# Stick-breaking attention weights: sigmoid(z) times a scanned product of sigmoid(-z), in place of exp(z minus a running sum of softplus)

## The chip, the cores and the metric

The kernel runs on one core of a Trainium2 chip. The metric is the device time of one execution in microseconds (us); less is better. A core has five engines that run beside each other and synchronise by semaphores: TensorE (PE, matrix products, with its own queue of weight loads, PEld), VectorE (DVE), ScalarE (ACT), GpSimd (POOL) and SyncE (SP, which issues the DMAs). Each engine runs its instructions in a fixed order.

## The reference

Two transformer-like blocks follow each other on 1024 tokens of width 1024, in float32. The second block projects its input to ten parts, among them q, k, v of a stick-breaking attention with 8 heads of width 128, and q, k, v of a retention; both results are gated, projected, merged and projected again. Only the stick-breaking attention matters here:

```python
z = jnp.einsum('bhqd,bhkd->bhqk', qi, k).astype(jnp.float32) * scale
qpos = i * Q_BLOCK + jnp.arange(Q_BLOCK)
mask = kpos[None, :] < qpos[:, None]
log_keep = jnp.where(mask, jax.nn.log_sigmoid(-z), 0.0)
suffix = lax.cumsum(log_keep, axis=3, reverse=True) - log_keep
w = jnp.where(mask, jnp.exp(jax.nn.log_sigmoid(z) + suffix), 0.0)
return jnp.einsum('bhqk,bhkd->bhqd', w.astype(v.dtype), v)
```

A query t gives the key s < t the weight sigmoid(z[t,s]) times the product of (1 - sigmoid(z[t,j])) over the keys j between s and t. Before attention q and k are normalised per head.

## The kernel before

The program is one long function, `tile_kernel`, written in the order of the computation; a scheduler with its own timeline then fixes the order of the instructions on every engine, so that work of neighbouring heads interleaves. Nearly every product is made of three passes, since float32 operands are split into a high and a low part: high x high, high x low, low x high (`PASSES`).

**The stages.** The first block takes the first part of the span. Then comes the stick-breaking stage, a loop over 8 heads, then one group of merge logits (`merge_logits(0)`), the retention with its own projections, the other merge logits, and the three final projections.

**A head of the stick-breaking stage** has two parts. The first is its projection: 8 weight tiles are loaded and split (`split_unit`: L67 and L68 on ACT and DVE for one half of the tiles, L70 and L71 on POOL for the other). `dense_tok` (L102) makes q, k and v for one block of 128 tokens after the other, 24 matmuls each of 384 columns, in a PSUM tile `acc`; there are three such banks. For every block of tokens ACT squares q and k with a running sum (L983), POOL makes the power -1/2 (`rsqrt_small`, L125 and L126), ACT and DVE split v (L986, L987) and DVE scales q and k into `sq` (L989). After four blocks PE transposes q and k (L996, eight transpositions into two of the `acc` banks), and ACT and DVE split the result into `qkt` (L1000, L1001). The gate of the head comes by `dense_col` (L112, 48 matmuls of 512 columns), or for head 0 in L1006.

The second part is attention proper, for two halves (`ib`) of 512 queries. The first half has four blocks on the diagonal, of 128, 256, 384 and 512 keys; the second half has four such blocks, and four off the diagonal with 512 keys each: 12 blocks in a head, 96 in all. For each block PE makes the logits `pz` (L1026, in one of two banks), ACT, DVE and POOL make the weights in the tile `A` (L1030 to L1051). They compute max(z, 0) + ln(1 + exp(-|z|)), which is softplus(z), its running sum from the last key to the first (the scan, L1042, whose start for off-diagonal blocks is a column `ini` of the diagonal one, L1046), then z minus that sum, and exp. On the diagonal a select sets the masked part, once before the scan and once after. When four blocks are there PE transposes the weights, in four groups by keys (L1058, into the banks `pt` and `pp` in turn), ACT casts a group to its high part (L1060), DVE subtracts it from the original for the low part (L1061), both called `wT`, and PE adds three products of the group to the output `po` (L1063), the first and third with the high part, the second with the low one. DVE copies `po` out (L1067).

The lines that the change touches:

```python
e1 = nc.scalar.activation(out=A[:, :w], in_=pz[:, :w], func=AF.Abs)
nc.scalar.copy(out=Z[:, :w], in_=pz[:, :w])
nc.scalar.activation(out=A[:, :w], in_=A[:, :w], func=AF.Exp, scale=-1.0)
nc.scalar.activation(out=A[:, :w], in_=A[:, :w], func=AF.Ln, bias=1.0)
```

ACT holds one set of function tables at a time. The program loads by hand the set with exp and ln (`load6`, L962), ordered behind the last SiLU of the first block; other loads are put in automatically where a function needs them.

## Time and profile before

| | |
|---|---|
| median of 3 runs | 2317.09 us (2314.77 to 2318.42) |
| the profiled execution | 2316.85 us |
| its span, first to last instruction | 2315.1 us |
| mean granted TensorE clock | 0.984 of full speed |
| PE busy | 2182.2 us, 94% of the span |
| DVE, POOL, ACT busy | 1242.6, 1210.2, 879.1 us (54%, 52%, 38%) |

The profile is of one execution. An engine's busy time is the sum of its instructions' time, overlaps counted once; its idle time is put down to what released the waiting instruction. Matmuls are pipelined, so that several are under way at a time: what one adds to the time is the distance from start to start, which is shorter than its duration. The granted clock of a stretch is a share of full speed, 2.4 GHz; the only other level is 1.2 GHz, so a share between 0.5 and 1 mixes the two. The stick-breaking stage lies at about 870 to 1437 us of the span.

### The profile page before, as it was taken

How to read it: one execution, taken by the hardware profiler on the slowest of the kernel's cores; microseconds unless marked ns; L12 is line 12 of the kernel's file. 1: busy time of each engine (PE TensorE's matmuls, PEld its weight loads, DVE VectorE, ACT ScalarE, POOL GpSimd, SP SyncE). 2: the span in 40 equal slices, each digit the busy share in tenths (PEclk: the TensorE clock that was granted, in tenths of full speed). 3: DMA queues.
4: the chain of work that ended last, by engine and by line, in shares of the span. 5: the costliest groups of instructions: out<-in, count | busy, mean ns of one | idle time of the engine just before them, and what ended most of it. 6: DMA issues, size and time to landing. Idle time of an engine off the chain costs nothing.

```text
span 2315.1 us, 33643 instructions
## 1 busy us (share of the span) xinstructions
PE 2182.2 (94%) x12197; PEld 1875.5 (81%) x12197; DVE 1242.6 (54%) x2228; ACT 879.1 (38%) x2191; POOL 1210.2 (52%) x1435
## 2 busy tenths in 40 slices
PE   7998888899999988999999999999989999999999
PEld 7777877787898778988888888788878788788887
DVE  4688789844457555665566453327474744321221
ACT  5344434445544225565566544012222222321200
POOL 6667778762004345554565545536575754434531
PEclk9999999999999999999999999999999999999999
DMA  4266830054486431110111103221324333644433
GB/s 129 83 165 166 206 86 26 35 159 130 146 280 215 147 106 42 55 47 23 51 51 55 51 32 97 67 69 55 125 87 132 95 105 101 218 164 152 142 106 107
DMA packets 238791, 249.25 MB, mean 108 GB/s; under 512 B 40032, under 2 KB 173856, under 8 KB 238368
## 3 DMA queue, kind: packets, MB, share of 16 engines
q1 hardware_dynamic: 238624, 247.10, 34.0%
q8 instruction: 96, 1.57, 0.3%
q14 instruction: 71, 0.58, 0.1%
HBM read 171.51 MB, written 75.53 MB: 107 GB/s over the span
## 4 chain that ended last, share of the span: by engine, by line
PE 43%; POOL 7%; DVE 7%; issue 4%; DMA 3%; ACT 3%; SPq 0%; POOLq 0%; ACTq 0%
PE acc L112 26%; PE acc L102 9%; PE acc L859 3%; POOL wu L71 2%; DMA raw<-in_w_in_dram 2%; PE po L1063 2%; DVE A L1042 1%; POOL wu L70 1%; DVE A L1037 1%; POOL A L1047 1%; PE pt L1179 1%; POOL ss L126 1%; ACT A L1036 1%; DVE xo L909 1%; DVE kf L132 1%
## 5 line engine op out<-in xcount | busy, mean ns | idle before, releaser
L112 PE MATMUL acc<-h2h,wu 128*128 128x512 f32 x1504 | 460.5, 396 | 0.7 <-POOL wu L71 0.4
L102 PE MATMUL acc<-wu,h2h 128*128 128x384 f32 (+1 forms) x1536 | 374.5, 326 | 11.5 <-DVE v L1117 5.5
L71 POOL TENSOR_TENSOR wu<-raw,wu 128x512 fp32r<-128x512 f32 (+3 forms) x268 | 364.9, 1370 | 6.1
L70 POOL TENSOR_SCALAR wu<-raw 128x512 fp32r<-128x512 f32 (+3 forms) x268 | 206.3, 773 | 269.1 <-PE acc L112 187.9
L112 PEld LDWEIGHTS acc<-h2h,wu 128*128 128x128 f32 x1504 | 281.8, 188 | 65.2 <-POOL wu L71 0.8
L102 PEld LDWEIGHTS acc<-wu,h2h 128*128 128x128 f32 x1536 | 270.4, 192 | 18.4 <-DVE v L1117 6.3
L112 PE MATMUL acc<-h2l,wu 128*128 128x512 f32 x752 | 277.9, 395 | 0.0
L102 PE MATMUL acc<-wu,h2l 128*128 128x384 f32 (+1 forms) x768 | 248.2, 324 | 0.0
L102 PE MATMUL acc<-wu,h1hi 128*128 128x384 f32 (+2 forms) x768 | 192.2, 334 | 12.7 <-DVE kS L518 6.7
L112 PE MATMUL acc<-h1hi,wu 128*128 128x512 f32 x512 | 164.5, 409 | 7.3 <-ACT pad L315 3.7
L112 PEld LDWEIGHTS acc<-h2l,wu 128*128 128x128 f32 x752 | 141.3, 188 | 31.0
L102 PEld LDWEIGHTS acc<-wu,h1hi 128*128 128x128 f32 x768 | 137.3, 195 | 17.0 <-issue 8.0
L102 PEld LDWEIGHTS acc<-wu,h2l 128*128 128x128 f32 x768 | 147.5, 192 | 1.3
L1047 POOL TENSOR_TENSOR A<-Z,A 128x128 f32<-128x128 f32 (+2 forms) x96 | 111.3, 1165 | 66.3 <-DVE A L1042 48.4
L125 POOL TENSOR_SCALAR ss<-ss 128x2 f32<-128x2 f32 (+2 forms) x136 | 40.7, 300 | 200.4 <-ACT sq L983 144.0
L102 PE MATMUL acc<-wu,h1lo 128*128 128x384 f32 (+2 forms) x384 | 126.8, 333 | 0.0
L112 PEld LDWEIGHTS acc<-h1hi,wu 128*128 128x128 f32 x512 | 98.2, 194 | 32.3 <-ACT pad L315 5.4
L126 POOL TENSOR_TENSOR ss<-ss,mhalf 128x2 f32<-128x2 f32 (+2 forms) x136 | 113.5, 835 | 8.3
L112 PE MATMUL acc<-h1lo,wu 128*128 128x512 f32 x256 | 96.2, 405 | 0.0
L1037 DVE SCALAR_TENSOR_TENSOR A<-Z,A 128x128 f32<-128x128 f32 (+2 forms) x96 | 70.4, 742 | 42.7 <-ACT A L1036 41.8
L1063 PE MATMUL po<-wT,v 128*128 128x512 f32 (+3 forms) x288 | 76.2, 362 | 14.0 <-DVE wT L1061 11.0
L320 DVE SCALAR_TENSOR_TENSOR cv<-pad,c_conv_w,cv 128x1024 f32<-128x1024 f32 x48 | 76.6, 1597 | 1.1
(549 smaller groups left out, 4685.1 us busy)
## 6 DMA issues: line engine op xcount, KB each, us to landing
raw<-in_w_in_dram SPq DMA_DIRECT2D x192, 256.0 KB, 3.0
d_pk<-sct SPq DMA_DIRECT2D x24, 512.0 KB, 4.3
raw<-in_w_out_dram SPq DMA_DIRECT2D x40, 256.0 KB, 2.9
wsa<-d_pk SPq DMA_DIRECT2D x16, 512.0 KB, 6.1
wsb<-d_pk SPq DMA_DIRECT2D x16, 512.0 KB, 7.1
d_sg<-lg SPq DMA_DIRECT2D x32, 256.0 KB, 2.9
sg<-d_sg SPq DMA_DIRECT2D x32, 256.0 KB, 3.4
raw<-in_w_in_dram SPq DMA_DIRECT2D x32, 192.0 KB, 2.7
```

The costliest lines, as they stand in the source:

```text
L70: nc.gpsimd.tensor_scalar(out=u[:, 0, :], in0=raw, scalar1=1.0, scalar2=0.0, op0=ALU.mult, op1=ALU.add)
L71: nc.gpsimd.tensor_tensor(out=u[:, 1, :], in0=raw, in1=f32(u[:, 0, :]), op=ALU.subtract)
L102: nc.tensor.matmul(acc[:, :n], lhsT=hT[a][:, k, m * P:(m + 1) * P], rhs=us[k][:, b, c0:c0 + n], start=(k == 0 and i == 0), stop=(k == NK - ...
L112: nc.tensor.matmul(accs[half], lhsT=us[k][:, b, c0:c0 + P], rhs=hT[a][:, k, half * 512:(half + 1) * 512], start=(k == 0 and i == 0), stop= ...
L125: nc.gpsimd.tensor_scalar(out=dst, in0=src, scalar1=mul, scalar2=eps, op0=ALU.mult, op1=ALU.add)
L126: nc.gpsimd.tensor_tensor(out=dst, in0=dst, in1=mhalf[:, :eshape], op=ALU.pow)
L132: nc.vector.transpose(out=dst[32 * b:32 * b + 32, :, :, 32 * a:32 * a + 32], in_=src[32 * a:32 * a + 32, :, :, 32 * b:32 * b + 32])
L320: nc.vector.scalar_tensor_tensor(out=cv, in0=pad[:, i:i + T], scalar=conv_w[:, blk, i:i + 1], in1=cv, op0=ALU.mult, op1=ALU.add)
L859: nc.tensor.matmul(acc, lhsT=us[k][:, y, (b % 4) * P:(b % 4 + 1) * P], rhs=token_set(mT[x][:, k, 0:T], s), start=(k == 0 and i == 0), stop ...
L1037: nc.vector.scalar_tensor_tensor(out=A[:, :w], in0=Z[:, :w], scalar=0.0, in1=A[:, :w], op0=ALU.max, op1=ALU.add)
L1047: nc.gpsimd.tensor_tensor(out=A[:, :w], in0=Z[:, :w], in1=A[:, :w], op=ALU.subtract)
L1063: nc.tensor.matmul(po[:, i0 * P:512], lhsT=v[a][:, c0 // P + kb, :], rhs=wT[b][:, :n], start=(diag and kb == 0 and x == 0), stop=(diag == ...
```

## The change

A block's weights are made from two sigmoids of the logits: `A` = sigmoid(-z) and `B` = sigmoid(z), each in one ACT pass out of PSUM. The tile `A` is one column longer, and POOL fills that column with 1. The scan now multiplies from the last key to the first (with a minimum against the same element, which changes nothing, as factors are at most 1), so that column s + 1 of `A` holds the product over the keys behind s; DVE multiplies `B` with it. The selects on the diagonal now set 1 in `A` and 0 in `B`, both before the scan. `A` has three buffers and `B` six, in place of six of `A` and three of `Z`. The manual table load is gone.

```diff
--- before.py
+++ after.py
@@ -959,9 +959,6 @@
     d_oa = dram.tile([8, P, T], F32, name="d_oa")
     d_ga = dram.tile([8, P, T], F32, name="d_ga")
     d_oag = dram.tile([8, P, T], F32, name="d_oag")
-    load6 = nc.scalar.add_instruction(mybir.InstLoadActFuncSet(name=nc.get_next_instruction_name(), act_func_set_id=6,
-                                                               ins=[], outs=[]))
-    after(load6, last_na[0])
     last_sb = None
     with tc.tile_pool(name="sb", bufs=1) as sb, tc.tile_pool(name="sr", bufs=1, side="right") as sr:
         gqk = sr.tile([P, 2, P], F32, name="gqk")
@@ -1026,30 +1023,25 @@
                             nc.tensor.matmul(pz[:, :w], lhsT=qk[0][a][:, i * P:(i + 1) * P], rhs=qk[1][b][:, c0:c0 + w],
                                              start=(x == 0), stop=(x == 2))
 
-                        A = sb.tile([P, 512], F32, tag="A", name="A", bufs=6)
-                        e1 = nc.scalar.activation(out=A[:, :w], in_=pz[:, :w], func=AF.Abs)
+                        A = sb.tile([P, 516], F32, tag="A", name="A", bufs=3)
+                        B = sb.tile([P, 512], F32, tag="B", name="B", bufs=6)
+                        e1 = nc.scalar.activation(out=A[:, :w], in_=pz[:, :w], func=AF.Sigmoid, scale=-1.0)
                         if h == 0:
-                            after(e1, load6)
-                        Z = sb.tile([P, 512], F32, tag="Z", name="Z", bufs=3)
-                        nc.scalar.copy(out=Z[:, :w], in_=pz[:, :w])
-                        nc.scalar.activation(out=A[:, :w], in_=A[:, :w], func=AF.Exp, scale=-1.0)
-                        nc.scalar.activation(out=A[:, :w], in_=A[:, :w], func=AF.Ln, bias=1.0)
-                        nc.vector.scalar_tensor_tensor(out=A[:, :w], in0=Z[:, :w], scalar=0.0, in1=A[:, :w],
-                                                       op0=ALU.max, op1=ALU.add)
+                            after(e1, last_na[0])
+                        last_sb = nc.scalar.activation(out=B[:, :w], in_=pz[:, :w], func=AF.Sigmoid)
+                        nc.gpsimd.memset(A[:, w:w + 1], 1.0)
                         if diag:
-                            nc.gpsimd.affine_select(out=A[:, w - P:w], in_=A[:, w - P:w], pattern=[[-1, P]],
-                                                    compare_op=ALU.is_gt, fill=0.0, base=0, channel_multiplier=1)
-                        nc.vector.tensor_tensor_scan(out=A[:, :w][:, ::-1], data0=A[:, :w][:, ::-1],
-                                                     data1=A[:, :w][:, ::-1], initial=0.0 if diag else ini[:, i4:i4 + 1],
-                                                     op0=ALU.add, op1=ALU.max)
+                            for t_, fill in ((A, 1.0), (B, 0.0)):
+                                nc.gpsimd.affine_select(out=t_[:, w - P:w], in_=t_[:, w - P:w], pattern=[[-1, P]],
+                                                        compare_op=ALU.is_gt, fill=fill, base=0, channel_multiplier=1)
+
+                        nc.vector.tensor_tensor_scan(out=A[:, :w + 1][:, ::-1], data0=A[:, :w + 1][:, ::-1],
+                                                     data1=A[:, :w + 1][:, ::-1], initial=1.0 if diag else ini[:, i4:i4 + 1],
+                                                     op0=ALU.mult, op1=ALU.min)
                         if diag and ib:
                             nc.vector.tensor_copy(out=ini[:, i4:i4 + 1], in_=A[:, 0:1])
-                        nc.gpsimd.tensor_tensor(out=A[:, :w], in0=Z[:, :w], in1=A[:, :w], op=ALU.subtract)
-                        if diag:
-                            nc.gpsimd.affine_select(out=A[:, w - P:w], in_=A[:, w - P:w], pattern=[[-1, P]],
-                                                    compare_op=ALU.is_gt, fill=NEG, base=0, channel_multiplier=1)
-                        last_sb = nc.scalar.activation(out=A[:, :w], in_=A[:, :w], func=AF.Exp)
-                        As.append(A)
+                        nc.vector.tensor_tensor(out=B[:, :w], in0=B[:, :w], in1=A[:, 1:w + 1], op=ALU.mult)
+                        As.append(B)
                     for kb in range(4):
                         i0 = kb if diag else 0
                         n = (4 - i0) * P
```

The scheduler gives the stick-breaking stage a new order on every engine; ahead of it ACT's table loads differ in one place, and behind it no order changes. In the rows below the names are those of the tiles, and a line of the changed kernel is up to eight lower than the same line before (L996 is L993, L1058 is L1050, L1061 is L1053, L1063 is L1055).

PE, where q and k of the first four token blocks of head 5 are transposed, among the output products of head 4's second half. `po<-wT,v` is an output product, `pt` and `pp` are transpositions of weights, `acc<-ident,sq` transpositions of q and k. Before:

```order
L102 MATMUL acc<-wu,h2l 128x384
L996 MATMUL acc<-ident,sq 128x128 x2
L1063 MATMUL po<-wT,v 128x512 x3
L1063 MATMUL po<-wT,v 128x384
L1058 MATMUL pt<-ident,A 128x128 x2
L1063 MATMUL po<-wT,v 128x384 x2
L1058 MATMUL pp<-ident,A 128x128
L996 MATMUL acc<-ident,sq 128x128 x4
L1063 MATMUL po<-wT,v 128x256 x3
L1058 MATMUL pt<-ident,A 128x128 x3
L1063 MATMUL po<-wT,v 128x128
L996 MATMUL acc<-ident,sq 128x128 x2
```

In the changed kernel:

```order
L102 MATMUL acc<-wu,h2l 128x384
L1055 MATMUL po<-wT,v 128x256 x2
L1055 MATMUL po<-wT,v 128x128
L1050 MATMUL pt<-ident,B 128x128
L1055 MATMUL po<-wT,v 128x128 x2
L1050 MATMUL pt<-ident,B 128x128 x3
L1050 MATMUL pp<-ident,B 128x128 x4
L993 MATMUL acc<-ident,sq 128x128 x6
L1055 MATMUL po<-wT,v 128x512 x4
L1050 MATMUL pt<-ident,B 128x128 x4
L993 MATMUL acc<-ident,sq 128x128 x2
L102 MATMUL acc<-wu,h2h 128x384 x2
```

Before, two groups of output products (512 and 384 columns) and part of a third stand between the first and the last transposition of q and k; now it is one product group and the first product of the next, and the groups of 256 and 128 columns stand ahead.

DVE at the same place: `wT<-pt,wT` and `wT<-pp,wT` are the low parts for which the second product of a group waits, `A<-A,ini` is the scan of an off-diagonal block, `A<-Z,A` the combination to softplus, `B<-B,A` the new multiplication. Before:

```order
L1037 SCALAR_TENSOR_TENSOR A<-Z,A 128x512
L1042 SCALAR_TENSOR_TENSOR A<-A,ini 128x512
L1037 SCALAR_TENSOR_TENSOR A<-Z,A 128x512
L1061 TENSOR_TENSOR wT<-pt,wT 128x512
L1042 SCALAR_TENSOR_TENSOR A<-A,ini 128x512
L1061 TENSOR_TENSOR wT<-pp,wT 128x384
L987 TENSOR_TENSOR v<-acc,v 128x128
L989 SCALAR_TENSOR_TENSOR sq<-acc,ss,gqk 128x128 x2
L1037 SCALAR_TENSOR_TENSOR A<-Z,A 128x512
L987 TENSOR_TENSOR v<-acc,v 128x128
L1061 TENSOR_TENSOR wT<-pt,wT 128x256
L1042 SCALAR_TENSOR_TENSOR A<-A,ini 128x512
```

In the changed kernel:

```order
L1038 SCALAR_TENSOR_TENSOR A<-A,ini 128x513
L1043 TENSOR_TENSOR B<-B,A 128x512
L984 TENSOR_TENSOR v<-acc,v 128x128
L1053 TENSOR_TENSOR wT<-pt,wT 128x256
L986 SCALAR_TENSOR_TENSOR sq<-acc,ss,gqk 128x128 x2
L1053 TENSOR_TENSOR wT<-pp,wT 128x128
L984 TENSOR_TENSOR v<-acc,v 128x128
L1053 TENSOR_TENSOR wT<-pt,wT 128x512
L986 SCALAR_TENSOR_TENSOR sq<-acc,ss,gqk 128x128 x2
L1053 TENSOR_TENSOR wT<-pp,wT 128x512
L1053 TENSOR_TENSOR wT<-pt,wT 128x512
L998 TENSOR_TENSOR qkt<-acc,qkt 128x512 x2
```

Before, scans and combinations alternate with the low parts, and the next row is `sq` of the fourth token block; now the two last scans and multiplications come first, and behind the low part of 256 columns no scan follows.

ACT at the first logits of head 0. Before:

```order
L1009 COPY gv<-acc 128x512
L1030 ACTIVATE A<-pz 128x128
L1034 COPY Z<-pz 128x128
L1030 ACTIVATE A<-pz 128x256
L1034 COPY Z<-pz 128x256
L1035 ACTIVATE A<-A 128x128
L67 CAST wu<-raw 128x512
L1035 ACTIVATE A<-A 128x256
L1036 ACTIVATE A<-A 128x128
L1036 ACTIVATE A<-A 128x256
```

In the changed kernel:

```order
L1006 COPY gv<-acc 128x512
L1028 ACT_TABLE_LOAD
L1028 ACTIVATE A<-pz 128x128
L1031 ACTIVATE B<-pz 128x128
L1028 ACTIVATE A<-pz 128x256
L1031 ACTIVATE B<-pz 128x256
L67 CAST wu<-raw 128x512 x2
L1028 ACTIVATE A<-pz 128x384
L1031 ACTIVATE B<-pz 128x384
```

A table load stands ahead of the first sigmoid. In the first block, behind the last SiLU, the change has an automatic load ahead of an Exp (L563) where the manual one stood.

## Rows read from the trace of the kernel before

**Rows 1.** Page, part 1: busy us (share of the span) and instructions.
```profile
span 2315.1 us, 33643 instructions
...
PE 2182.2 (94%) x12197; PEld 1875.5 (81%) x12197; DVE 1242.6 (54%) x2228; ACT 879.1 (38%) x2191; POOL 1210.2 (52%) x1435
```

**Rows 2.** Stretches: from:to, length, busy us of each engine, clock, DMA, GB/s.
```profile
870.00:1437.00 567.00, 536.78 (x2917) 484.41 (x2916) 316.45 (x571) 322.94 (x949) 305.06 (x421) 0.99 0.15 47
...
885.00:900.00 15.00, 15.00 (x83) 13.96 (x82) 7.71 (x11) 8.07 (x22) 11.32 (x14) 1.00 0.43 127
...
1134.60:1203.90 69.30, 65.48 (x366) 59.78 (x365) 39.79 (x74) 40.82 (x123) 36.91 (x53) 1.00 0.15 46
```

**Rows 3.** Waits of PE, 850 to 1450 us: us in total, times, longest.
```profile
PE acc L996 <- DVE sq L989: 13.8, 11, 4.9
PE po L1063 <- DVE wT L1061: 11.0, 14, 1.4
PE pz L1026 <- ACT Z L1034: 4.1, 7, 0.8
```

**Rows 4.** Timeline of PE, head 5: start, us, instruction, [idle before, releaser].
```profile
1198.22 0.90 PE L1063 MATMUL po<-wT,v 128*128 128x512 f32 x3 [0.98 <-DVE wT L1061]
...
1199.87 0.62 PE L1063 MATMUL po<-wT,v 128*128 128x384 f32 x2 [0.52 <-DVE wT L1061]
...
1200.43 0.70 PE L996 MATMUL acc<-ident,sq 128*128 128x128 f32 x4
...
1201.92 0.51 PE L1063 MATMUL po<-wT,v 128*128 128x256 f32 x2 [0.68 <-DVE wT L1061]
...
1203.35 0.59 PE L996 MATMUL acc<-ident,sq 128*128 128x128 f32 x2 [0.54 <-DVE sq L989]
```

**Rows 5.** Timeline of the other engines at the same place.
```profile
1195.73 1.30 POOL L1047 TENSOR_TENSOR A<-Z,A 128x512 f32<-128x512 f32 x1 [2.01 <-DVE A L1042]
...
1195.94 1.63 DVE L1037 SCALAR_TENSOR_TENSOR A<-Z,A 128x512 f32<-128x512 f32 x1 [0.36 <-ACT A L1036]
...
1196.06 0.58 ACT L1060 CAST wT<-pt 128x512 fp32r<-128x512 f32 x1
...
1197.49 0.68 DVE L1061 TENSOR_TENSOR wT<-pt,wT 128x512 fp32r<-128x512 f32 x1
...
1198.09 1.27 DVE L1042 TENSOR_TENSOR_SCAN A<-A,ini 128x512 f32<-128x512 f32 x1
```

**Rows 6.** Stretches with a lower clock (columns as in rows 2).
```profile
916.00:925.00 9.00, 5.68 (x22) 5.30 (x20) 4.01 (x10) 6.06 (x13) 2.42 (x4) 0.66 0.00 0
...
1337.00:1342.00 5.00, 2.23 (x7) 1.63 (x7) 4.37 (x7) 3.86 (x12) 4.71 (x4) 0.68 0.00 0
1342.00:1347.00 5.00, 4.80 (x27) 4.41 (x26) 3.02 (x8) 1.96 (x7) 2.16 (x3) 0.64 0.00 0
```

**Rows 7.** Groups: instruction, count, busy us, mean ns, idle before and releaser.
```profile
L1036 ACT ACTIVATE A<-A 128x128 f32<-128x128 f32 (+2 forms) x96 | 52.6, 564 | 0.2
...
L1051 ACT ACTIVATE A<-A 128x128 f32<-128x128 f32 (+2 forms) x96 | 52.1, 547 | 64.0 <-POOL A L1049 41.6 <-POOL A L1047 22.3
...
L1047 POOL TENSOR_TENSOR A<-Z,A 128x128 f32<-128x128 f32 (+2 forms) x96 | 111.3, 1165 | 66.3 <-DVE A L1042 48.4
...
L1037 DVE SCALAR_TENSOR_TENSOR A<-Z,A 128x128 f32<-128x128 f32 (+2 forms) x96 | 70.4, 742 | 42.7 <-ACT A L1036 41.8
```

**Rows 8.** Single lines (ns min/median/max), and a group of fills.
```profile
L1239 ACT ACTIVATE sg<-sg x32: 616/632/637, 1998.2 to 2218.0; 128x512 f32<-128x512 f32 x32
...
L1239 ACT ACT_TABLE_LOAD  x1: 1283/1283/1283, 1996.9 to 1996.9; - x1
...
L68 DVE TENSOR_TENSOR wu<-raw,wu x44: 658/791/1565, 725.0 to 1316.8; 128x512 fp32r<-128x512 f32 x44
...
L313 POOL MEMSET pad<- 128x2 f32 x12 | 1.2, 102 | 0.0
```

**Rows 9.** Chain that ended last, in order of time: start, us, what.
```profile
1203.94 3.33 PE acc L102 x19
```

## Prediction

> **What bounds the kernel now.** The page's first part comes first: TensorE (PE) is busy for 2182.2 of 2315.1 us, 94%, and no other engine passes 54% [rows 1]. So the end is set by PE's work plus the time in which PE stands idle or runs at a lower clock, and taking work off ScalarE (ACT), VectorE (DVE) or GpSimd (POOL) is worth only what it takes out of PE's idle time. The order of PE's instructions outside the stick-breaking stage is the same before and after; so I look at that stage alone. Its window from 870 to 1437 us holds 536.8 us of PE work, so 30.2 us idle [rows 2]; a head in the steady state (69.3 us) holds 65.5, so 3.8 us idle. 30.2 us is 1.3% of the span: with what the clock loses (below) that is all the change can win.
>
> Next, who PE waited for: in and just ahead of that window 13.8 us for `sq` (L989, DVE) before the transpositions L996, 11.0 us for the low half `wT` (L1061, DVE) before the output products L1063, 4.1 us for `Z` (ACT) to release a logits bank [rows 3]. The timeline says where: in head 5 four waits of 0.98, 0.52, 0.68 and 0.54 us, 2.7 us in all, stand within 7 us [rows 4]. I call this the cluster. There the first four tokens' q and k of a head are transposed (L996), few dense matmuls are ready, and the previous head's output products have to fill the gap; every one of the seven heads after the first has such a place.
>
> Then what PE waits for there. DVE is hardly ever idle: a softplus combination (L1037) takes 1.63 us beside a POOL subtraction of 1.30 us, only then comes the first `wT` subtraction (0.68), then a scan of 1.27 us, then the next `wT` [rows 5]. The waits are queueing on DVE, behind long attention operations that PE doesn't need yet.
>
> The granted clock is the last view: 0.99 over the stage [rows 2], but 0.66 in 916 to 925 us and 0.68 and 0.64 in 1337 to 1347 us, stretches in which PE had stood idle for about 3 us [rows 6]. A share of 0.66 is a mix of the two levels, 1.2 and 2.4 GHz. Lost: 9 x 0.34 + 5 x 0.32 + 5 x 0.36 = 6.5 us. Together 36.7 us lie open in the stage.
>
> **The change, part by part.** It runs 96 times (12 blocks in each of 8 heads).
>
> ACT: of five passes (Abs, Copy, Exp, Ln, Exp) two sigmoids remain. Ln takes 52.6 us and the last Exp 52.1 [rows 7]; the first Exp, on the same tiles, is put at the same, so some 157 us go. A sigmoid of 128x512 takes 632 ns in the later merge gates, much as these passes [rows 8]. ACT is no bound here; off PE's path this is worth nothing. What it gives is that a block's chain gets shorter and that ACT's queue holds nothing between a transposition and its cast.
>
> POOL: the subtraction goes, 96 x 1165 ns = 111 us [rows 7], and with it the collisions with DVE. Both masks stay two selects. 96 one-column fills come; a fill of two columns took 102 ns [rows 8], so 10 us. POOL is no bound.
>
> DVE: the combination goes, 70.4 us busy [rows 7]; a multiplication comes. The nearest row for two SBUF operands at width 512 is L68, 658 ns at the least, 791 median, 1565 at worst [rows 8]; the combination took up to 1.63 in the cluster. I take 0.7: without POOL's subtraction it will mostly run undisturbed. The bounds are 0.66 and 1.57, the second no better than now, on the engine PE waits for. The multiplication's second operand starts at the tile's second word. The Trainium skill, Vector Engine (DVE) Microarchitecture Reference, section Measured stream behaviour on trn2, measured 1.30 instead of 1.054 ns per column for pairs that start on an odd word; by it 0.66 would be 0.81 us, and no row here has such an operand. The scan keeps its form with one element more: 1.27 us at width 512 [rows 5]; mult and min in place of add and max are shown by no row. I take the same and keep both sides: down to a plain pass (0.66), up to twice (2.5).
>
> Tables: the manual load in the first part goes, but its place is taken by an automatic one for that part's Exp, and one more is put ahead of the first sigmoid: plus 1283 ns on ACT [rows 8]. Cover: from 885 to 900 us PE works without a gap [rows 2], and the block's chain after it is shorter by three ACT passes. If the cover were gone it would cost 1.3 us. The Trainium skill, ScalarE: Activation LUTs, section What ACT_TABLE_LOAD costs, adds a drain of 1.38 us to the load; the rows show no such record, and by it the term would be 2.7 us at most.
>
> The order is what pays. At head 5's cluster PE had two groups of output products, with their low halves, between the first and the last L996. Now one group of four lies there, and the low halves of the 256 and 128 groups are done before. On DVE a scan stood between one `wT` subtraction and the next; now the last four subtractions follow the `sq` pairs with no scan or multiplication between them. Walked through with rows: behind the new cluster's transpositions into `pt` PE has four into `pp`, six L996 and one product, by 0.70 us for four transpositions [rows 4] about 1.9 us, until it needs the first low half; the chain to that is a cast of 0.58 and a subtraction of 0.68 [rows 5], 1.3 us, plus up to 1 us if ACT squares the fourth token first. So 0 to 0.7 us remains, 0.6 taken, in place of 2.7. At worst (the chain comes late as now) all 2.7 remain.
>
> **Sum.** What remains idle: 0.6 in each of six clusters, 3.6; 3 in head 1's, where several product groups still stand among the L996 (it lost over 4); the bank waits for the second ACT pass, 0.6 x 7 = 4.2, since two passes read a bank before and after; 1.8 in head 0 before attention begins; 2 for `sq` ahead of L102. That is 14.6 of 30.2: 15.6 us won. Of the clock's 6.5 us I give back 4.5, as the 3 us gaps shrink. Less 1.3 for the table at worst: 18.8. The profiled execution took 2316.85 us (span 2315.1); 2316.85 - 18.8 = **2298**. The median of the three runs, 2317.09, differs from it by 0.2 us, so the same number is taken for the median. The bounds of the forecast itself: all waits in the clusters and all of the clock's loss gone, 2288; half of it, 2307.
>
> **Rivals.** About 0.2% (4.6 us) is what a measurement of this kernel can tell from no change.
>
> 1. The waits move. The scans still take 1.27 us, and three or four of them stand on DVE ahead of the 512 and 384 subtractions of the second diagonal block's first products. If the order that is fixed beforehand counts them too short, PE waits there, outside the cluster. For: the waits now arise just so, behind a scan. Against: from the block's last transposition to the low half PE has 23 dense matmuls there, by 3.33 us for 19 some 4.0 us [rows 9], and six logits matmuls of 0.3 each [rows 4]. One wait of 1.6 us in each of seven heads takes 11 of the 19 us: 2309.
>
> 2. No change. The last L996 of a cluster waits for a chain which the edit does not touch: square on ACT, POOL's power, `sq` on DVE, the 13.8 us [rows 3]. If that chain sets the cluster's length, PE will only wait in another row. For: it is the largest item. Against: on DVE the fourth block's `sq` stood behind a scan, and no longer does. Then only a few us of the cluster go, and a table load comes: 2315.
>
> 3. Slower: the product scan. DVE multiplies each element into a running value. A scan of 512 takes 1.27 us where a plain two-operand pass takes 0.66 [rows 5, 8], so its pace is set by feedback from element to element; a slower feedback for a product would stretch 96 scans. Point of decision: 18.8 us over seven heads is 2.7 per head, and about 1 us of slack covers more; four off-diagonal scans must grow by 0.9 us each, to 2.2 us. At 2.5 us they grow by 4.9 us per head, 3.9 beyond the slack, so (3.9 - 2.7) x 7 = 8 us lost: 2325, and more if gaps of 3 us pull the clock down again. For: no row shows a product scan. Against: the number of operations per element is the same.
>
> **How the numbers follow.** Forecast 60%, rival 1 17%, rival 2 13%, rival 3 10%. Faster by over 0.2%: forecast and rival 1, 0.77; within: 0.13; slower: 0.10. The forecast alone would span 2288 to 2307. The range for 8 in 10 goes on to 2317 for rival 1 and most of rival 2, and down to 2286 for a scan that is a little quicker; it leaves out the slower case, a third of rival 2 and a few per cent at the low end.
>
> **What would show it.** Right: a head's period of about 67 us in place of 69.3; waits for `wT` before the output products under 5 us; no DVE operation of over 1.5 us in the clusters; no window of 5 us in a cluster with a clock under 0.9, but for head 1's; ACT busy about 150 us less, POOL about 100 less. Wrong: a scan row at 2 us or more (rival 3); `sq` still at 13 us or more (rival 2); waits at L1063 that lie among dense matmuls (rival 1); a change of time outside the stage, where no order has moved.

## The result, and the profile after

| | before | after |
|---|---|---|
| median, 4 runs each | 2316.31 us (2314.77 to 2318.42) | 2284.99 us (2281.08 to 2287.59) |
| profiled execution | 2316.85 us | 2281.08 us |
| its span | 2315.1 us | 2279.4 us |

The ratio after to before is 0.9863, 95% interval 0.9848 to 0.9877: faster by 31.3 us. The sign was forecast; the time lies 1 us under the range of 2286 to 2317, and the gain is 1.7 times the forecast 18.8 us. The profiled execution after is the fastest of its four and the one before lies near the median, so the two profiles differ by 35.8 us, 4.5 more than the medians.

The page's first part after (answers to [rows 1]):

```profile
span 2279.4 us, 33389 instructions
...
PE 2171.1 (95%) x12197; PEld 1872.3 (82%) x12197; DVE 1222.5 (54%) x2228; ACT 763.6 (33%) x1904; POOL 1107.4 (49%) x1435
```

PE has the same 12197 matmuls and is busy 11 us less. ACT lost 115 us and POOL 103, and neither number is the gain. The next two fences are stretches between the same two instructions ahead of and behind the stick-breaking stage, before and after (columns as in [rows 2]); the last line is a head after.

```profile
863.71:1453.90 590.19, 559.97 (x3025) 504.39 (x3025) 317.75 (x573) 325.57 (x957) 317.31 (x434) 0.99 0.17 53
```

```profile
861.76:1419.20 557.44, 549.75 (x3028) 501.24 (x3027) 300.51 (x573) 209.87 (x670) 215.43 (x433) 1.00 0.18 56
...
1023.93:1089.01 65.08, 64.40 (x366) 59.61 (x365) 38.56 (x74) 26.15 (x87) 24.45 (x52) 1.00 0.16 49
```

The stage is 32.75 us shorter: nearly the whole difference lies in it. PE's idle time falls from 30.22 to 7.69 us (22.5), its busy time from 559.97 to 549.75 (10.2) for the same work. A steady head takes 65.08 us in place of 69.30 [rows 2], with 0.7 us idle and full clock. One place with a lower clock is left, in head 0 ahead of attention:

```profile
880.00:885.00 5.00, 4.41 (x14) 3.32 (x15) 2.48 (x7) 1.31 (x3) 2.27 (x4) 0.66 0.01 3
```

PE's waits in the stage after (answers to [rows 3], whose window begins earlier: 6.0 of its 13.8 us for `sq` lie ahead of the stage):

```profile
PE pz L1023 <- ACT B L1031: 4.2, 7, 0.6
PE acc L993 <- DVE sq L986: 1.7, 2, 1.6
PE po L1055 <- DVE wT L1053: 1.3, 1, 1.3
```

Of the 14 waits for low halves one is left, in head 1; the logits bank waits are as they were, and of the 1.7 us for `sq` all lie in head 0. In a steady head's cluster PE doesn't wait at all. Timeline of PE, and then of DVE, in head 5 after (answer to [rows 4, 5]):

```profile
1180.01 0.51 PE L1050 MATMUL pt<-ident,B 128*128 128x128 f32 x3
1180.36 0.60 PE L1050 MATMUL pp<-ident,B 128*128 128x128 f32 x4
1180.80 0.82 PE L993 MATMUL acc<-ident,sq 128*128 128x128 f32 x6
1181.37 1.52 PE L1055 MATMUL po<-wT,v 128*128 128x512 f32 x4
1182.73 0.60 PE L1050 MATMUL pt<-ident,B 128*128 128x128 f32 x4
1183.16 0.38 PE L993 MATMUL acc<-ident,sq 128*128 128x128 f32 x2
```

```profile
1175.33 1.28 DVE L1038 TENSOR_TENSOR_SCAN A<-A,ini 128x513 f32<-128x513 f32 x1
1176.71 0.69 DVE L1043 TENSOR_TENSOR B<-B,A 128x512 f32<-128x512 f32 x1
...
1180.48 0.29 DVE L984 TENSOR_TENSOR v<-acc,v 128x128 fp32r<-128x128 f32 x1 [1.82 <-ACT v L983]
1181.18 0.69 DVE L1053 TENSOR_TENSOR wT<-pt,wT 128x512 fp32r<-128x512 f32 x1 [0.41 <-ACT wT L1052]
```

The last scan and multiplication are over at 1177.4 us; at the low half of the next 512-column group DVE is idle and waits for ACT's cast alone. No row of PE in the cluster carries a bracket, the mark of a wait.

The new operations, by group:

```profile
L1038 DVE TENSOR_TENSOR_SCAN A<-A,ini 128x513 f32<-128x513 f32 x32 | 41.0, 1280 | 1.3 <-ACT A L1028 1.2
L1043 DVE TENSOR_TENSOR B<-B,A 128x512 f32<-128x512 f32 x48 | 33.1, 690 | 3.1 <-ACT B L1031 0.5
...
L1032 POOL MEMSET A<- 128x1 f32 x96 | 8.4, 97 | 26.3 <-DVE B L1043 23.5 <-DVE h2l L911 1.8 <-DVE ini L1042 0.5
```

The scan takes 1.28 us (1.27 expected), the multiplication 0.69 (0.7), the fill 97 ns (102). The signs that were named for the forecast are there but for one, and go further: a period of 65 us where 67 was named, 1.3 us of waits for low halves where under 5 was. The exception is ACT, whose busy time fell by 115 us where about 150 was named.

### The profile page after: what moved, and what is told of

Same layout as the page of the kernel before. It is cut to its first block, busy times and chain, and to the rows that moved or that the text cites. A ratio compares the mean times of both kernels' runs of the same rounds, so it can differ in the third digit from the quotient of the medians.

```text
span 2279.4 us, 33389 instructions
## 1 busy us (share of the span) xinstructions
PE 2171.1 (95%) x12197; PEld 1872.3 (82%) x12197; DVE 1222.5 (54%) x2228; ACT 763.6 (33%) x1904; POOL 1107.4 (49%) x1435
## 4 chain that ended last, share of the span: by engine, by line
PE 54%; POOL 5%; issue 3%; DMA 2%; DVE 2%; ACT 1%; SPq 0%; POOLq 0%; ACTq 0%
PE acc L112 29%; PE acc L102 13%; PE acc L859 3%; PE po L1055 2%; PE pz L1023 2%; POOL wu L71 1%; POOL wu L70 1%; PE pt L1050 1%; PE pt L1171 1%; DMA d_oag<-oa 1%; DMA oa<-d_oa 1%; PE acc L1003 1%; POOL ob L1202 1%; PE pp L1050 0%; PE acc L120 0%
## 5 line engine op out<-in xcount | busy, mean ns | idle before, releaser
L102 PE MATMUL acc<-wu,h2h 128*128 128x384 f32 (+1 forms) x1536 | 370.0, 324 | 6.8 <-DVE v L1109 4.0
L102 PEld LDWEIGHTS acc<-wu,h2h 128*128 128x128 f32 x1536 | 268.0, 191 | 12.7 <-DVE v L1109 4.9
L102 PE MATMUL acc<-wu,h2l 128*128 128x384 f32 (+1 forms) x768 | 246.0, 321 | 0.0
L102 PE MATMUL acc<-wu,h1hi 128*128 128x384 f32 (+2 forms) x768 | 192.0, 333 | 12.6 <-DVE kS L518 6.7
L102 PEld LDWEIGHTS acc<-wu,h1hi 128*128 128x128 f32 x768 | 137.1, 195 | 17.0 <-issue 8.0
L102 PEld LDWEIGHTS acc<-wu,h2l 128*128 128x128 f32 x768 | 146.1, 190 | 1.9
L102 PE MATMUL acc<-wu,h1lo 128*128 128x384 f32 (+2 forms) x384 | 126.7, 333 | 0.0
L126 POOL TENSOR_TENSOR ss<-ss,mhalf 128x2 f32<-128x2 f32 (+2 forms) x136 | 119.2, 877 | 8.6
L980 ACT ACTIVATE sq<-acc 128x128 f32<-128x128 f32 x128 | 35.6, 289 | 128.5 <-PE acc L102 124.4
L112 PE MATMUL acc<-oah,wu 128*128 128x512 f32 x256 | 76.9, 396 | 0.0
L1055 PE MATMUL po<-wT,v 128*128 128x512 f32 (+3 forms) x288 | 74.7, 351 | 1.7 <-DVE wT L1053 1.3
```

The source lines that it names most:

```text
L102: nc.tensor.matmul(acc[:, :n], lhsT=hT[a][:, k, m * P:(m + 1) * P], rhs=us[k][:, b, c0:c0 + n], start=(k == 0 and i == 0), stop=(k == NK - ...
L112: nc.tensor.matmul(accs[half], lhsT=us[k][:, b, c0:c0 + P], rhs=hT[a][:, k, half * 512:(half + 1) * 512], start=(k == 0 and i == 0), stop= ...
L126: nc.gpsimd.tensor_tensor(out=dst, in0=dst, in1=mhalf[:, :eshape], op=ALU.pow)
L980: nc.scalar.activation(out=sq[:, a * P:(a + 1) * P], in_=acc[:, a * P:(a + 1) * P], func=AF.Square, accum_out=ss[:, a:a + 1])
L1055: nc.tensor.matmul(po[:, i0 * P:512], lhsT=v[a][:, c0 // P + kb, :], rhs=wT[b][:, :n], start=(diag and kb == 0 and x == 0), stop=(diag == ...
```

## The experiments

The change does three things at once: it gives PE a new order, it shortens a block's chain (ACT's Exp and Ln and DVE's combination ahead of the scan, POOL's subtraction and ACT's Exp behind it), and it unloads ACT and POOL. The theory on record was the first. e3 and e4 are edits of the changed kernel with every order the scheduler's. In the other kernels here PE's order of the stage was fixed by edges between its matmuls, to the list of one of the two kernels; the orders of the other engines were the scheduler's in every run, so a part of a difference may be what it made of the edit. The edges:

```diff
+    pe_order = [pe_log[a + x] for a, n in json.loads(zlib.decompress(base64.b85decode(PE_ORDER))) for x in range(n)]
+    for earlier, later in zip(pe_order, pe_order[1:]):
+        after(later, earlier)
```

In the kernels with a fixed order all matmuls carry the lines of a helper, L49 and L55. A table first; each ratio is to runs of the kernel before from the same session, and the stretch is from the first copy of `po` to the last in the profiled execution (some 2646 matmuls in each). Lost clock is the sum over pieces of 3 us of their length times what the clock lacks to 1.

| run | ratio to before, 95% | stretch | PE idle in it | lost clock |
|---|---|---|---|---|
| before | 1 | 509.1 | 24.1 | 3.4 |
| new order, new arithmetic (after) | 0.9863 | 481.0 | 5.9 | 0.0 |
| e1 old order, new arithmetic | 0.9860 (0.9834 to 0.9886) | 481.0 | 6.0 | 0.0 |
| e2 new order, old arithmetic | 1.0438 (1.0413 to 1.0462) | 610.2 | 96.4 | 46.0 |
| e3 multiplication on POOL | 0.9863 (0.9835 to 0.9891) | 484.6 | 6.2 | 1.7 |
| e4 one sigmoid | 0.9866 (0.9842 to 0.9890) | 484.6 | 5.8 | 1.7 |
| f1 e1 + 3 ACT passes ahead of the scan | 0.9950 (0.9934 to 0.9965) | 503.8 | 18.9 | 5.1 |
| f2 e1 + 3 ACT passes that nothing waits for | 0.9869 (0.9851 to 0.9887) | 486.8 | 8.7 | 1.7 |
| f3 e1 + 1 POOL pass that nothing waits for | 1.0000 (0.9985 to 1.0014) | 508.7 | 24.9 | 5.1 |
| f4 before, subtraction on DVE | 1.0020 (1.0007 to 1.0033) | 517.8 | 26.8 | 10.2 |
| g1 e1 + 1 DVE pass ahead of the scan | 0.9938 (0.9915 to 0.9960) | 494.5 | 16.9 | 0.0 |
| g2 f1 + DVE pass ahead, multiplication on POOL | 0.9978 (0.9962 to 0.9994) | 511.1 | 19.9 | 15.4 |
| g3 the whole old chain rebuilt | 1.0021 (1.0007 to 1.0034) | 513.1 | 26.2 | 5.1 |
| h1 e1 + 3 ACT passes beside the scan | 0.9849 (0.9830 to 0.9867) | 480.0 | 4.6 | 0.0 |

### Is it the order?

e1 keeps the changed kernel's arithmetic and fixes PE to the order of the kernel before.

> The changed kernel (sigmoids and a scanned product), with PE's order in the stick-breaking stage held to the one of the kernel before by extra order edges between neighbouring matmuls; the other engines' orders stay free. Theory O (the new PE order is what pays): the old clusters come back, with two groups of output products between the first and the last transposition of q and k, so low-half waits of about 8 to 11 us and a head's period of 68 to 69 us; 2305 to 2316 us. Theory Q (the shorter queues pay: no combination on DVE, no subtraction on POOL beside it, three ACT passes fewer; the order is incidental): the low halves come early even in the old order, period 65 to 66 us, 2283 to 2292 us.

Median 2288.61 us, ratio 0.986: all of the gain, in the old order. The kernel before, then e1:

```profile
928.00:1437.10 509.10, 484.98 (x2645) 436.95 (x2644) 287.78 (x514) 293.10 (x853) 275.85 (x375) 0.99 0.15 48
```

```profile
928.00:1409.00 481.00, 474.99 (x2645) 434.59 (x2644) 272.09 (x513) 185.76 (x593) 181.90 (x370) 1.00 0.16 51
```

e2 is the opposite, the old arithmetic in the new order.

> The kernel before (softplus, running sum, exp), with PE's order in the stick-breaking stage held to the one of the changed kernel. Theory O: most of the gain stays, 2285 to 2297 us. Theory Q: the old chain of five ACT passes, combination, scan and subtraction is too long for an order that asks for the weights sooner, so PE waits for transposed weights and low halves, and the time is 2316 us or more, perhaps 2330.

Median 2420.89 us, 4.4% slower than before. Its waits of PE in the stage:

```profile
PE pt L55 <- ACT A L1071: 92.6, 29, 6.8
```

The new order asks for the transposition of a block's weights earlier, and with the old chain PE waits there for its last Exp, up to 6.8 us at a time. So the order wins nothing by itself; by my reading it is what the scheduler can afford once the chain is short. Within the changed kernel it is worth nothing that these runs can tell: the stretch takes 481.0 us in either order, with 2.8 us of waits for low halves in e1 (5 waits) and 1.3 after, and less for logits banks in e1 (3.2 against 4.2).

### Is it a single part of the new arithmetic?

e3 puts the multiplication on POOL, where the old subtraction stood:

```diff
-                        nc.vector.tensor_tensor(out=B[:, :w], in0=B[:, :w], in1=A[:, 1:w + 1], op=ALU.mult)
+                        nc.gpsimd.tensor_tensor(out=B[:, :w], in0=B[:, :w], in1=A[:, 1:w + 1], op=ALU.mult)
```

> The changed kernel with the multiplication of the two sigmoid parts on POOL in place of DVE. It takes about 62 us of work from DVE in the stage and puts about 110 us on POOL, where the subtraction was. If DVE's load is what made PE wait, nothing is lost: 2283 to 2287 us. If POOL's part in the chain (1.2 us per block, and its collisions with DVE's two-operand passes and scans) was the trouble, a good part of the 31 us comes back: 2295 to 2305 us.

Median 2287.38 us, ratio 0.9863: a two-operand pass on POOL behind the scan costs nothing that the times can tell. e4 makes `A` as 1 - `B` on POOL, so that one ACT pass reads each logits bank:

```diff
-                        e1 = nc.scalar.activation(out=A[:, :w], in_=pz[:, :w], func=AF.Sigmoid, scale=-1.0)
...
+                        nc.gpsimd.tensor_scalar(out=A[:, :w], in0=B[:, :w], scalar1=-1.0, scalar2=1.0, op0=ALU.mult, op1=ALU.add)
```

> The changed kernel with one sigmoid only: B = sigmoid(z) from ACT, masked by one select, and A = 1 - B by POOL. A logits bank is read by one ACT pass in place of two, so the seven waits of 0.6 us for a bank should go: 4 us less than the changed kernel, 2281 us. The rival: POOL's pass of about 0.8 us per block lengthens the chain before the scan and collides with DVE, and PE waits for weights: 2287 us or more.

Median 2288.45 us, ratio 0.9866, no better. That is the rival's time without its wait: PE waited 0.3 us for weights. The bank waits fell only from 4.2 to 3.1 us, and one wait of 2.5 us for `sq` in head 1 stands in the place of the 1.3 us for a low half. There are 6 us of PE's idle time to win, and neither run won them.

### Is it the load or the chain?

These add work to e1, so PE's order is the old one. f1 adds three passes on ACT that change nothing but stand in the chain:

```diff
                         last_sb = nc.scalar.activation(out=B[:, :w], in_=pz[:, :w], func=AF.Sigmoid)
+                        for _ in range(3):
+                            nc.scalar.copy(out=A[:, :w], in_=A[:, :w])
```

> New math in PE's old order (as the run before that gave 2289 us), and the factor tile A goes through three more ACT copies in place before the scan, so that ACT has five passes per block again and the chain before DVE's first step is as long as with Abs, Exp and Ln. Theory ACT (DVE stood blocked because its next operation waited for a late ACT pass, with the low halves queued behind it): the waits for low halves come back, 8 us or more, and the time is 2305 to 2320 us. Theory POOL (the collision of POOL's two-operand subtraction with DVE's combination stretched DVE's queue): the time stays at 2285 to 2293 us.

Median 2305.79 us: of e1's gain of 1.40% 0.90 points are gone. PE's waits for low halves are back, 11.6 us over 14 waits (2.8 in e1, 11.0 over 14 before). The same cluster in e1 and in f1, first DVE in e1:

```profile
1048.40 1.28 DVE L1058 TENSOR_TENSOR_SCAN A<-A,ini 128x513 f32<-128x513 f32 x1
1049.82 0.69 DVE L1063 TENSOR_TENSOR B<-B,A 128x512 f32<-128x512 f32 x1
...
1050.63 0.68 DVE L1073 TENSOR_TENSOR wT<-pt,wT 128x512 fp32r<-128x512 f32 x1
...
1051.74 0.55 DVE L1073 TENSOR_TENSOR wT<-pp,wT 128x384 fp32r<-128x384 f32 x1
```

The last scan of the head is over before the first low half; PE's 512-column products at 1052.44 us follow without a wait. DVE in f1, then PE in f1:

```profile
1046.60 1.29 DVE L1060 TENSOR_TENSOR_SCAN A<-A,ini 128x513 f32<-128x513 f32 x1 [0.63 <-ACT A L1053]
...
1048.58 0.68 DVE L1075 TENSOR_TENSOR wT<-pt,wT 128x512 fp32r<-128x512 f32 x1
...
1050.24 1.28 DVE L1060 TENSOR_TENSOR_SCAN A<-A,ini 128x513 f32<-128x513 f32 x1
...
1051.62 0.68 DVE L1065 TENSOR_TENSOR B<-B,A 128x512 f32<-128x512 f32 x1
1052.22 0.42 DVE L1075 TENSOR_TENSOR wT<-pt,wT 128x256 fp32r<-128x256 f32 x1
```

```profile
1049.32 0.91 PE L49 MATMUL po<-wT,v 128*128 128x512 f32 x3 [1.08 <-DVE wT L1075]
...
1050.83 0.27 PE L55 MATMUL pp<-ident,B 128*128 128x128 f32 x1
1050.94 0.60 PE L55 MATMUL acc<-ident,sq 128*128 128x128 f32 x4
...
1052.69 0.57 PE L49 MATMUL po<-wT,v 128*128 128x256 f32 x3 [1.03 <-DVE wT L1075]
```

DVE stands still at a scan until ACT's copy is done, and a scan and a multiplication that should have been over by then come between the low halves: the pattern of [rows 5]. f2 puts the same three passes on a scratch tile, where nothing waits for them:

```diff
+                            after(nc.scalar.copy(out=scr[:, :w], in_=scr[:, :w]), last_sb)
```

> New math in PE's old order, with three more ACT passes per block on a scratch tile that nobody waits for: ACT's load without the longer chain. Theory ACT by load: 2300 us or more. Theory ACT by chain, and theory POOL: 2285 to 2295 us.

Median 2287.04 us, ratio 0.9869: ACT's load costs nothing that the times can tell from e1. In the profiled executions the stretch is 5.8 us longer than e1's, 1.7 of them clock, so a small part of f1's 22.8 us may be load. h1, the last run, leaves the three copies on ACT in the chain of the weights, but on `B`, which is wanted behind the scan:

```diff
+                            nc.scalar.copy(out=B[:, :w], in_=B[:, :w])
```

> The run with three ScalarE copies in place on A gave 2305.8 us. Here the same three copies stand on B in place of A, so the scan no longer waits for them, only the multiplication behind the scan: ScalarE has as much to do and its queue holds as many passes ahead of the casts, but they lie beside the scan (1.28 us) and lengthen a block's chain by about 0.5 x 3 - 1.3 = 0.2 to 0.6 us in place of 1.5 to 1.9. If the length of the chain to the weights counts: 2288 to 2295 us, waits for low halves under 5 us. If the passes cost through ScalarE's queue (casts of wT and squares stand behind them): 2300 to 2308, waits for low halves and for sq over 15 us together, as when they stood on A.

Median 2282.97 us, ratio 0.9849: nothing lost, and less time than either theory gave. Stretches in f1, then in h1:

```profile
922.30:1426.10 503.80, 484.93 (x2645) 438.71 (x2644) 275.48 (x512) 291.55 (x851) 178.54 (x370) 0.99 0.15 48
```

```profile
922.50:1402.50 480.00, 475.42 (x2646) 434.71 (x2645) 272.39 (x513) 289.86 (x851) 176.08 (x371) 1.00 0.16 51
```

Instructions and busy time of ACT are alike, 851 and 290 us; 23.8 us of time lie between them. It matters whether the scan has to wait for the passes, and hardly how many there are.

g1 lengthens the chain on DVE instead:

```diff
+                        nc.vector.tensor_tensor(out=A[:, :w], in0=A[:, :w], in1=A[:, :w], op=ALU.max)
```

> The sigmoids' arithmetic in the old order of the matmuls, and one VectorE pass more for every block, in place on A, between the sigmoids and the scan (the maximum of A and A, which is A): VectorE's queue gets three passes a block in place of two, ScalarE's chain stays at two. New order alone: 2288.6; with three ScalarE passes more: 2305.8. Theory 1 (a block's chain ahead of its scan is what counts, ScalarE's part and VectorE's part of it alike): one pass of 0.69 us against three of about 0.6 us, so a third to a half of the 17 us, 2293 to 2298, with waits of about 4 us for low halves. Theory 2 (VectorE's queue is the thing, since the low halves stand in it): more than the ScalarE passes cost, 2305 to 2320, waits for low halves over 11 us. Theory 3 (only ScalarE's chain counts, because VectorE stands still while it lasts): 2289 to 2291.

Median 2302.91 us: 0.78 points gone for one pass of 0.69 us a block, between the times of theories 1 and 2, and more than I had put on the chain. Waits for low halves: 12.3 us in 7 waits, as theory 2 had them, fewer and longer than in f1. By my reading a DVE pass ahead of the scan counts twice, since it lengthens the chain and stands in the queue of the low halves; no run parts the two.

f4 goes at the old kernel from the other side, with the subtraction taken off POOL:

```diff
-                        nc.gpsimd.tensor_tensor(out=A[:, :w], in0=Z[:, :w], in1=A[:, :w], op=ALU.subtract)
+                        nc.vector.tensor_tensor(out=A[:, :w], in0=Z[:, :w], in1=A[:, :w], op=ALU.subtract)
```

> The kernel before in its own PE order, with the subtraction of the running sum moved from POOL to DVE. It takes 111 us off POOL and the collisions with them, and puts some 62 us on DVE. Theory POOL: a good part of the gain comes with it, 2290 to 2305 us. Theory ACT: nothing is won, and DVE's longer queue costs: 2315 to 2330 us.

Median 2321.57 us, ratio 1.002. The combination's 512-column form fell from 925 to 696 ns on average, so collisions with POOL were real and are gone there; the time didn't move. Waits of PE in f4:

```profile
PE po L49 <- DVE wT L1081: 13.3, 8, 2.6
PE acc L55 <- DVE sq L1009: 5.0, 4, 2.4
```

For `sq` PE waited 5.0 us in place of 10.9, for low halves 13.3 in place of 11.0, for ACT's casts and last Exp 6.6 in place of 3.4, and the stretch lost 6.8 us more of clock than before. That DVE's queue, a pass longer, stands behind the longer waits is my reading. f3 adds a two-operand POOL pass on scratch to e1:

```diff
+                        after(nc.gpsimd.tensor_tensor(out=scr[:, :w], in0=scr[:, :w], in1=scr[:, :w], op=ALU.subtract), one)
```

> New math in PE's old order, with one two-operand subtraction per block on a scratch tile added to POOL: POOL's old load and its collisions with DVE's two-operand multiplication and scan, without the longer chain. Theory POOL: DVE's multiplication is stretched to 1.5 us in the clusters and low-half waits come back, 2300 us or more. Theory ACT: 2285 to 2293 us.

Median 2317.34 us, ratio 1.0000: all of the gain gone, but by another wait. Waits of PE in f3:

```profile
PE acc L55 <- DVE sq L1008: 16.7, 9, 2.4
PE po L49 <- DVE wT L1076: 4.2, 6, 0.9
```

and POOL in f3 ahead of the 2.36 us wait that ends at 1088.44 us:

```profile
1085.85 0.82 POOL L1055 TENSOR_TENSOR scr<-scr 128x384 f32<-128x384 f32 x1
1086.62 0.34 POOL L1058 TENSOR_SCALAR_AFFINE_SELECT B<-B 128x128 f32<-128x128 f32 x1
1086.94 1.05 POOL L145 TENSOR_TENSOR ss<-ss,mhalf 128x2 f32<-128x2 f32 x1
```

The power that `sq` needs (L145) stands in POOL's queue behind the scratch pass and selects. Low halves are hardly late (4.2 us). DVE, too, was busier in the stretch than in e1 (298.85 us against 272.09), with off-diagonal scans of 1.50 us on average in place of 1.29. So f3 doesn't rebuild the old loss; it shows that POOL too has a queue in which PE's next work can get stuck. In e3, though in the new order, as many POOL passes stand behind the scans, the off-diagonal scans are as slow (1.50 us), and the time is that of the changed kernel.

### Can the old loss be rebuilt?

g2 is f1 with g1's pass in front as well and the multiplication on POOL, so that DVE has no more passes than before:

> The sigmoids' arithmetic in the old order of the matmuls, three ScalarE copies in place on A (as in the run with 2305.8) and behind them one VectorE pass in place on A, both ahead of the scan; the multiplication goes to POOL, so VectorE has two passes a block, as in the kernel before and in the run with 2305.8. Theory 1 (the chain ahead of the scan): longer than in that run by one VectorE pass in front and 0.6 us more behind (1.3 us on POOL for 0.69 us on VectorE), 2311 to 2320, waits for low halves and for sq over 25 us together. Theory 2 (the number of VectorE passes): the same number, so 2303 to 2308. Theory 3 (only ScalarE's chain): 2303 to 2308 as well, with the waits for low halves at about 12 us.

Median 2314.16 us, as the chain theory had it; low halves and `sq` were waited for 19.5 us, not 25, and 15.4 us of clock were lost. g3 goes on to the whole old shape:

```diff
+                        for _ in range(2):
+                            nc.scalar.copy(out=A[:, :w], in_=A[:, :w])
+                        nc.vector.tensor_tensor(out=A[:, :w], in0=A[:, :w], in1=A[:, :w], op=ALU.max)
...
+                        nc.gpsimd.tensor_tensor(out=B[:, :w], in0=B[:, :w], in1=A[:, 1:w + 1], op=ALU.mult)
+                        last_sb = nc.scalar.copy(out=B[:, :w], in_=B[:, :w])
```

> The sigmoids' arithmetic in the old order of the matmuls, with the old chain rebuilt out of passes that change nothing: two sigmoids and two copies on ScalarE, one pass on VectorE, the scan, the multiplication on POOL in the place of the old subtraction, and a last copy on ScalarE in the place of the old last Exp. Every engine has as many passes a block as in the kernel before (the select of a diagonal block apart), and only the functions differ. If the shape of the chain is all: 2313 to 2320, the times of the kernel before, with waits for low halves near 11 us and for sq near 11 us. If something of the old functions themselves (their table, the form of the combination, whose 512 columns took 0.925 us on average) carries part of the loss: 2295 to 2310.

Median 2323.04 us, ratio 1.0021: the time of the kernel before, and 0.2% more. PE's waits in g3:

```profile
PE po L49 <- DVE wT L1077: 12.6, 16, 1.7
PE pz L49 <- ACT B L1051: 6.5, 10, 0.9
PE acc L55 <- DVE sq L1006: 5.3, 4, 2.7
```

They are those of the kernel before in kind, with 16 waits for low halves where there were 14, less for `sq` (8.0 us with its second row, where there were 10.9) and more for logits banks (6.5, where there were 4.1). So the functions (Exp, Ln, sums in place of products) aren't needed for the loss; passes that change nothing bring it back. What each pass is worth stays open, as they don't add up: f1 returns 0.90 points, g1 0.78, and g2, which has both and the multiplication on POOL, 1.18.

## Why the prediction was right and wrong

**What bounds the kernel: right.** The difference lay in PE's lost time in this one stage (32.75 of 35.8 us in the profiled executions), and PE's clusters are where it was won.

**"The order is what pays": wrong, and it is the step that failed.** The part on ACT had said that a shorter chain is what the passes give, then priced it at nothing and looked for the gain in the order's rows. e1 has the old rows on PE and the whole gain; e2 has the new rows and loses 4.4%; f1 brings 0.90 of the 1.40 points back with late scans alone, and g3 all of them with the whole chain. What the low halves had queued behind were scans that came late, since ACT's four passes and DVE's own combination stood ahead of them. Take these away and the scans are over before the cluster's low halves in either order. Two rows told it: DVE's new order (scans first, then low halves), where I read a list as a cause that by e1 it is not, and [rows 7], where DVE stands idle ahead of its combination for 42.7 us, 41.8 of them for ACT's Ln. DVE is full in the cluster itself, as the prediction says, but with work that came late. So the sign came out right by a term that the prediction had put at nothing.

**Sizes of the sum.** In the order of the text; measured is the stage of the two profiled executions:

| term | forecast | measured |
|---|---|---|
| idle in six steady clusters | 3.6 left | 0 |
| head 1's cluster | 3 left | 1.3 |
| logits bank waits | 4.2 left | 4.2 |
| head 0 ahead of attention | 1.8 left | 1.7 |
| `sq` ahead of L102 | 2 left | 0 |
| idle won, of 30.2 | 15.6 | 22.5 |
| clock won | 4.5 | about 3.8 |
| busy time not of the clock | not seen | about 6.4 |
| table load | -1.3 | 0 |
| sum | 18.8 | 32.7 |

The terms that put the time under the range are the idle time, 6.9 us more of it won, and the busy time, which the sum didn't have. Since the chains are short, nothing in the steady heads is late any more but the logits banks.

The clock's part was sized by a mistake: 6.5 us were counted over whole stretches, in which PE also stood idle. By PE's busy time in them [rows 6] it is 5.68 x 0.34 + 2.23 x 0.32 + 4.80 x 0.36 = 4.4; counted in pieces of half a microsecond, which also take in the edges of the stretches, 5.5. Not all of it was won: those two places are at full clock after, but 1.7 us are lost in the new one at 880 us. That leaves 3.8.

The rest of the 10.2 us of busy time, 6.4, I had not thought of. A likely reading is that a matmul ahead of a wait counts as busy until its modelled end, while in a dense run the next one has started by then: in the rows of f1 a transposition takes 0.27 us and the next one starts 0.11 us behind it, so by an estimate a wait adds some 0.16 us of busy time, 5 us for 32 waits fewer (42 to 10 in the stage). No run measures this by itself, and it isn't a fixed price: g1 has 14 waits in its stretch to e1's 10, no clock lost in either, and 2.6 us more busy time. With it and the idle time the stage had some 42 us to win, not 36.7.

The table load took 1283 ns, as said, and PE worked through it:

```profile
889.63 1.28 ACT L1028 ACT_TABLE_LOAD   x1
890.92 0.28 ACT L1028 ACTIVATE A<-pz 128x128 f32<-128x128 f32 x1
```

**Parts priced right, and one not.** Scan, multiplication and fill came out within 5%, and POOL lost 103 us (about 100 were named). ACT lost 115, not 150: the durations of its passes fell by 158 us (five passes of 255.2 against two of 97.1), but busy time counts overlaps once, and successive passes overlap (the sigmoid that starts at 890.92 us takes 0.28, and the next one starts 0.18 behind it). Neither load by itself is worth time that the runs can tell (f2, e3).

**Rivals.** Rival 1 (waits behind scans among dense matmuls) didn't come: one wait for a low half is left. Rival 2 named the `sq` chain as untouched; its waits in the stage fell from 10.9 us (7.8 before the transpositions, 3.1 before L102) to 1.7. In the stage before:

```profile
PE acc L996 <- DVE sq L989: 7.8, 8, 3.3
...
PE acc L102 <- DVE sq L989: 3.1, 6, 0.8
```

By my reading `sq` no longer queues on DVE behind late scans; but DVE's own wait for POOL's power ahead of `sq` also fell, from 25.6 to 12.8 us over the whole kernel, and f4, with less work on POOL, halved the waits for `sq` as well. No run parts the two. Rival 3 needed a scan of 2.2 us; it takes 1.28.

**The range** ended at 2286. The bound of 2288 let the waits of the clusters and the clock's loss go but kept the other waits at full size, and it had no term for busy time.

## What to carry to other kernels

When PE waits for a short operation that queues behind a long one, look at what the long one itself waited for: an in-order engine that stands at a late operation holds up everything behind it, so passes ahead of that operation cost time though their engine has time to spare (f1 against h1: the same passes on ACT, which is busy for six tenths of the stretch, 23.8 us apart). A new instruction order that comes with an edit is no cause until a run with the old order says so. And idle time in a profile can understate what waits cost: here 6.4 us of busy time went with them.

## What the runs showed of the hardware that was not expected

The scan takes as long multiplying and comparing (1.28 us for 513 columns) as adding and comparing (1.27 for 512). The multiplication whose second operand starts at the second word of its tile took 690 ns for 512 columns on average, as much as g1's pass of the same width with both operands at the first word, 694 ns. The Trainium skill, Vector Engine (DVE) Microarchitecture Reference, section Measured stream behaviour on trn2, gives 1.30 in place of 1.054 ns a column for pairs that start on an odd word in both sources; here one source does, so its case, which the prediction applied to one operand, isn't tested, and one such operand shows no price. Nor do the rows around the table load show the drain of 1.38 us that the Trainium skill, ScalarE: Activation LUTs, section What ACT_TABLE_LOAD costs, adds: the copy ahead of it starts at 889.03 us and takes 0.59, and the sigmoid starts 1.29 us after the load's start.

The clock fell after some waits and not after others. In head 0 PE has the same two waits for `sq` before and after (1.56 and 0.19 us, 1.55 and 0.18); the 6 us that begin where the first ends had a granted clock of 1.00 before and of 0.72 after. In f1 PE was busy for 2.13 of 4.30 us, and the next 6 us had a granted clock of 0.72; in g1 it was busy for 0.80 of 3.26 us, a longer gap in one piece, and the next 6 us stood at 1.00. f1, then g1:

```profile
1119.00:1123.30 4.30, 2.13 (x15) 1.51 (x14) 4.29 (x10) 1.70 (x8) 2.24 (x2) 1.00 0.00 0
1123.30:1129.30 6.00, 5.72 (x30) 5.43 (x29) 2.03 (x4) 1.17 (x2) 0.00 (x0) 0.72 0.00 0
```

```profile
1053.00:1056.26 3.26, 0.80 (x5) 0.45 (x4) 3.16 (x6) 0.78 (x5) 1.25 (x2) 1.00 0.00 0
1056.26:1062.26 6.00, 6.00 (x38) 5.75 (x39) 3.58 (x10) 1.71 (x4) 0.00 (x0) 1.00 0.00 0
```

What decides it stays open; in the stretch of the table g1's 16.4 us of named waits lost no clock at all, g2's 19.8 us lost 15.4.
